# Sum of absolute differences: absolute sums moved to ScalarE, the last row cut into column pieces, six buffers

## The chip, the cores and the metric

The kernel runs on one core of one Trainium2 chip. The metric is the device time of one execution in microseconds (us). TensorE does no work in this kernel; what matters are the transfers from HBM (the chip's main memory) into SBUF (the core's working memory of 128 partitions), VectorE (DVE in the rows), ScalarE (ACT) and SyncE (SP). DMAs can be issued from SP and from ACT; each has a queue of its own, SPq and ACTq in the rows, and the packets of both run on the core's 16 DMA engines.

## The reference

Two float32 arrays of 1024 x 4096 are subtracted, and the absolute differences are summed along each row. The result is one float32 for each of the 1024 rows.

```python
batch, dim = 1024, 4096          # x, y: float32, axis = -1
return np.sum(np.abs(x - y), axis=axis).astype(np.float32)
```

The inputs are 2 x 16.78 MB, the output 4 KB.

## The kernel before

The 1024 rows are laid over the 128 partitions, eight to each partition. The loop (line 29) runs over these eight slots. The text calls a slot a "row": row 0 to row 7, each a tile of 128 x 4096 of x and one of y, 2 MB apiece.

For each row, SP issues the transfer of the x tile (line 33) and ACT that of the y tile (line 34). VectorE subtracts in place, tx = tx - ty (line 35), and then sums the absolute values of tx along the free dimension into one column of `ro` (line 36). After the loop SP writes `ro` out (line 38). ScalarE computes nothing; only its queue is used.

The pools for x and y have four buffers each (lines 23 and 24), so the first four rows are issued at once and the transfer of row 4 has to wait until row 0 has been used: its y transfer until the subtraction has read ty, its x transfer until the absolute sum has read tx. The order on VectorE is made by a scheduler that does not keep the order of the loop: it puts two subtractions and then two sums, as the rows of VectorE's order further down show.

Of the kernel before, what the change touches and what calls it, by code (L numbers as in the profile page):

```python
# [5 lines left out]

KCS = [1]*8

@with_exitstack
def kernel(ctx, tc, x, y, axis, out):  # L10
    nc = tc.nc
    P = nc.NUM_PARTITIONS
    R, C = x.shape
    K = R // P
    xr = x.rearrange("(p k) c -> p k c", p=P, k=K)
    yr = y.rearrange("(p k) c -> p k c", p=P, k=K)
    orr = out.rearrange("(p k) -> p k", p=P, k=K)
    kcs = KCS
    assert sum(kcs) == K
    pools = {}  # L20
    for kc in set(kcs):
        pools[kc] = (
            ctx.enter_context(tc.tile_pool(name=f"px{kc}", bufs=4)),
            ctx.enter_context(tc.tile_pool(name=f"py{kc}", bufs=4)),
        )
    with tc.tile_pool(name="pr", bufs=1) as poolr:
        ro = poolr.tile([P, K], mybir.dt.float32)
        o = 0
        for kc in kcs:
            poolx, pooly = pools[kc]  # L30
            tx = poolx.tile([P, kc, C], x.dtype)
            ty = pooly.tile([P, kc, C], y.dtype)
            nc.sync.dma_start(out=tx, in_=xr[:, o:o+kc, :])
            nc.scalar.dma_start(out=ty, in_=yr[:, o:o+kc, :])  # L34
            nc.vector.tensor_sub(out=tx, in0=tx, in1=ty)  # L35
            nc.vector.reduce_sum(out=ro[:, o:o+kc], in_=tx, axis=mybir.AxisListType.X, apply_absolute_value=True)  # L36
            o += kc
        nc.sync.dma_start(out=orr, in_=ro)


# [1 line left out]
_INS = ['x', 'y', 'axis']  # L42
_OUTS = [((1024,), 'float32')]
#: Inputs that are plain numbers.
_NUMBERS = {'axis': -1}


def kernel(**inputs):
    import numpy as _np
    import concourse.bacc as _bacc  # L50
    import concourse.tile as _tile
    from concourse import mybir as _mybir
    from concourse.bass_utils import run_bass_kernel_spmd as _run

    nc = _bacc.Bacc("TRN2", target_bir_lowering=False, num_devices=1)  # L55
    arrays, args = {}, []
    for name in _INS:
        if name in _NUMBERS:
            args.append(_NUMBERS[name])
            continue  # L60
        a = _np.ascontiguousarray(inputs[name])
        if a.dtype.kind in "iu":
            a = a.astype(_np.int64)
        arrays[f"in_{name}_dram"] = a
        args.append(nc.dram_tensor(f"in_{name}_dram", a.shape, _mybir.dt.from_np(a.dtype), kind="ExternalInput").ap())
    for i, (shape, dtype) in enumerate(_OUTS):
        dt = _mybir.dt.from_np(_np.dtype(dtype))
        args.append(nc.dram_tensor(f"out_{i}_dram", shape, dt, kind="ExternalOutput").ap())
    with _tile.TileContext(nc) as tc:
        kernel(tc, *args)  # L70
    r = _run(nc, [arrays], core_ids=[0])
    got = tuple(r.results[0][f"out_{i}_dram"] for i in range(len(_OUTS)))
    return got[0]
```

## Time and profile before

| | |
|---|---|
| median of 3 runs | 97.60 us (97.56 to 97.62) |
| span of the profiled execution, first to last instruction | 95.8 us |
| VectorE busy | 69.9 us, 73% of the span, 16 instructions |
| one subtraction / one absolute sum of 128 x 4096 | 4.42 us / 4.41 us |
| bytes read from HBM | 33.55 MB |
| rate of the transfers while they run | 424 to 433 GB/s |

The whole time of the profiled execution is not listed apart from the three runs, which lie within 0.06 us. It is taken as their median: 97.6 us, of which the span is 95.8 us, and the other 1.8 us lie around the span.

A row of the profile names the line, the engine, the operation and its tiles. Idle time of an engine is put down to what ended it. The time of a DMA "to landing" runs from its issue to the moment at which its semaphore says that all of it is there.

### The profile page before, as it was taken

What the parts mean: (1) busy time and instruction counts of PE and PEld (TensorE: products, weight loads), DVE (VectorE), ACT (ScalarE), POOL (GpSimd) and SP (SyncE); (2) the same over time, 40 slices, a digit from 0 to 9 for tenths busy, and PEclk for the clock granted to TensorE, in tenths of its full rate; (3) what the DMA queues carried; (4) which work ended last, traced back from release to release, by engine and by line L of the source; (5) the groups of instructions that cost most, each with busy time, mean ns of one, the idle gap of its engine ahead of it and who ended that gap; (6) DMA issues with size and microseconds to landing.
All of it is one profiled execution on the core that took longest, in us unless ns stands there. A gap on an engine that the chain in (4) does not pass through costs nothing.

```text
span 95.8 us, 95 instructions
## 1 busy us (share of the span) xinstructions
DVE 69.9 (73%) x16; POOL 0.2 (0%) x4
## 2 busy tenths in 40 slices
DVE  0000069996930499999982999999909999999990
POOL 0000000000000000000000000000000000000000
DMA  4899999999999999999999999999999995000000
GB/s 109 369 431 424 424 438 438 438 431 438 431 424 438 424 417 431 431 411 431 438 438 424 431 431 431 424 424 424 431 411 438 438 438 212 0 0 0 0 0 2
DMA packets 2448, 33.56 MB, mean 350 GB/s; under 512 B 400, under 2 KB 400, under 8 KB 400
## 3 DMA queue, kind: packets, MB, share of 16 engines
q1 hardware_dynamic: 1296, 16.78, 41.7%
q10 hardware_dynamic: 1152, 16.78, 41.1%
HBM read 33.55 MB, written 0.00 MB: 350 GB/s over the span
## 4 chain that ended last, share of the span: by engine, by line
DMA 68%; DVE 24%; issue 4%; ACTq 1%
DMA ty<-in_y_dram 68%; DVE tx L35 14%; DVE ro L36 10%; ACTq L34 1%
## 5 line engine op out<-in xcount | busy, mean ns | idle before, releaser
L35 DVE TENSOR_TENSOR tx<-tx,ty 128x4096 f32<-128x4096 f32 x8 | 35.4, 4422 | 23.6 <-DMA ty<-in_y_dram 23.6
L36 DVE TENSOR_REDUCE ro<-tx 128x1 f32<-128x4096 f32 x8 | 35.1, 4413 | 0.1
L55 POOL MEMSET const-bfloat16-1.0<- 128x1 bf16 x1 | 0.1, 103 | 0.0
L55 POOL MEMSET const-uint8-127<- 128x1 uint8 x1 | 0.1, 103 | 0.0
L55 POOL MEMSET const-float32-1.0<- 128x1 f32 x1 | 0.1, 100 | 0.0
L55 POOL MEMSET const-float32-0.0<- 128x1 f32 x1 | 0.1, 99 | 0.2 <-issue 0.2
## 6 DMA issues: line engine op xcount, KB each, us to landing
ty<-in_y_dram ACTq DMA_DIRECT2D x8, 2048.0 KB, 33.1
tx<-in_x_dram SPq DMA_DIRECT2D x8, 2048.0 KB, 23.6
out_dram<-ro SPq DMA_DIRECT2D x1, 4.0 KB, 1.4
```

The costliest lines, as they stand in the source:

```text
L34: nc.scalar.dma_start(out=ty, in_=yr[:, o:o+kc, :])
L35: nc.vector.tensor_sub(out=tx, in0=tx, in1=ty)
L36: nc.vector.reduce_sum(out=ro[:, o:o+kc], in_=tx, axis=mybir.AxisListType.X, apply_absolute_value=True)
L55: nc = _bacc.Bacc("TRN2", target_bir_lowering=False, num_devices=1)
```

## The change

VectorE now only subtracts. The absolute sums of whole rows are ScalarE activations with the function Abs, which also accumulate along the free dimension into a column of `ro`. The pools have six buffers. The order is the order of the code (`manual_schedule`): loads of rows 0 to 3, then for each row the load of the row four ahead, the subtraction and the absolute sum.

Row 7 is cut into column pieces of 2304, 1152, 512 and 128. All eight of its transfers (x and y of each piece) are issued on SP's queue. Each of the first three pieces is subtracted on VectorE and summed on ScalarE into one of three columns of a small tile `last`. The fourth piece, 128 columns, is subtracted into the same tile beside these three columns, and one VectorE reduction over the 131 columns of `last` gives the sum of row 7.

```diff
-KCS = [1]*8
+PIECES = [2304, 1152, 512, 128]
...
-            ctx.enter_context(tc.tile_pool(name=f"px{kc}", bufs=4)),
-            ctx.enter_context(tc.tile_pool(name=f"py{kc}", bufs=4)),
...
+    px = ctx.enter_context(tc.tile_pool(name="px", bufs=6))
+    py = ctx.enter_context(tc.tile_pool(name="py", bufs=6))
+    ps = ctx.enter_context(tc.tile_pool(name="ps", bufs=1))
+    with tc.manual_schedule():
+        ro = ps.tile([P, K], F32, tag="ro")
+        last = ps.tile([P, n_part + PIECES[-1]], F32, tag="last")
...
+            if k < K - 1:
+                nc.sync.dma_start(out=tx, in_=xr[:, k, :])
+                nc.scalar.dma_start(out=ty, in_=yr[:, k, :])
+                return
+            o = 0
+            for w in PIECES:
+                nc.sync.dma_start(out=tx[:, o:o + w], in_=xr[:, k, o:o + w])
+                nc.sync.dma_start(out=ty[:, o:o + w], in_=yr[:, k, o:o + w])
+                o += w
...
+            nc.vector.tensor_sub(out=tx, in0=tx, in1=ty)
+            nc.scalar.activation(tx, tx, ABS, accum_out=ro[:, k:k + 1])
...
+        for k in range(4):
+            load(k)
+        for k in range(K - 1):
+            if k + 4 < K:
+                load(k + 4)
+            whole(k)
...
-            nc.vector.tensor_sub(out=tx, in0=tx, in1=ty)
-            nc.vector.reduce_sum(out=ro[:, o:o+kc], in_=tx, axis=mybir.AxisListType.X, apply_absolute_value=True)
...
+        for i, w in enumerate(PIECES):
+            s = slice(o, o + w)
+            if i < n_part:
+                nc.vector.tensor_sub(out=tx[:, s], in0=tx[:, s], in1=ty[:, s])
+                nc.scalar.activation(tx[:, s], tx[:, s], ABS, accum_out=last[:, i:i + 1])
+            else:
+                nc.vector.tensor_sub(out=last[:, n_part:n_part + w], in0=tx[:, s], in1=ty[:, s])
+                nc.vector.reduce_sum(out=ro[:, K - 1:K], in_=last, axis=AX, apply_absolute_value=True)
```

VectorE's order before, from row 0 to the end. A name with DMAHW in the brackets is a semaphore that counts landed DMAs; DVE and Activation are the semaphores of VectorE and ScalarE.

```order
L35 TENSOR_TENSOR tx<-tx,ty 128x4096
L36 TENSOR_REDUCE ro<-tx 128x1
L35 TENSOR_TENSOR tx<-tx,ty 128x4096 x2
L36 TENSOR_REDUCE ro<-tx 128x1 x2
L35 TENSOR_TENSOR tx<-tx,ty 128x4096 x2
L36 TENSOR_REDUCE ro<-tx 128x1 x2
L35 TENSOR_TENSOR tx<-tx,ty 128x4096 x2
L36 TENSOR_REDUCE ro<-tx 128x1 x2
L35 TENSOR_TENSOR tx<-tx,ty 128x4096
L36 TENSOR_REDUCE ro<-tx 128x1
```

Behind the last subtraction but one stand two sums, and only then the subtraction and the sum of row 7. VectorE's order in the change, from the subtraction of row 6 to the end:

```order
L50 TENSOR_TENSOR tx<-tx,ty 128x4096 [waits DMAHW5_49,DMAHW4_49,Activation_49]
L64 TENSOR_TENSOR tx<-tx,ty 128x2304 [waits DMAHW7_49,DMAHW6_49,Activation_49]
L64 TENSOR_TENSOR tx<-tx,ty 128x1152 [waits DMAHW1_49,DMAHW0_49]
L64 TENSOR_TENSOR tx<-tx,ty 128x512 [waits DMAHW3_49,DMAHW2_49]
L67 TENSOR_TENSOR last<-tx,ty 128x128 [waits DMAHW5_49,DMAHW4_49]
L68 TENSOR_REDUCE ro<-last 128x1 [waits DVE_49,Activation_49]
```

The sums are gone from VectorE up to the last reduction, which now waits for ScalarE. ScalarE's order in the change, behind the first four issues of y transfers (before, it had eight issues of y transfers and nothing else):

```order
L40 DMA ty_85<-in_y_dram 128x4096 [waits DMAHW0_49]
L51 ACT_TABLE_LOAD
L51 ACTIVATE tx_68,ro_66<-tx_68 128x4096 [waits DVE_49]
L40 DMA ty_91<-in_y_dram 128x4096 [waits DMAHW3_49]
L51 ACTIVATE tx_72,ro_66<-tx_72 128x4096 [waits DVE_49]
L40 DMA ty_97<-in_y_dram 128x4096 [waits DMAHW5_49]
...
L51 ACTIVATE tx_96,ro_66<-tx_96 128x4096 [waits DVE_49]
L65 ACTIVATE tx_102,last_67<-tx_102 128x2304 [waits DVE_49]
L65 ACTIVATE tx_102,last_67<-tx_102 128x1152 [waits DVE_49]
L65 ACTIVATE tx_102,last_67<-tx_102 128x512 [waits DVE_49]
```

tx_68 is row 0, tx_72 row 1, tx_96 row 6 and tx_102 row 7; the y transfers shown are those of rows 4, 5 and 6. The issues of rows 5 and 6 now stand behind an activation. SP's order in the change, behind the x transfers of rows 0 to 5 (before, it had eight transfers of 128 x 4096 and the output):

```order
L39 DMA tx<-in_x_dram 128x4096 [waits DMAHW4_49,Activation_49]
L44 DMA tx<-in_x_dram 128x2304 [waits DMAHW6_49,Activation_49]
L45 DMA ty<-in_y_dram 128x2304 [waits DMAHW7_49,DVE_49]
L44 DMA tx<-in_x_dram 128x1152 [waits DMAHW0_49]
L45 DMA ty<-in_y_dram 128x1152 [waits DMAHW1_49]
L44 DMA tx<-in_x_dram 128x512 [waits DMAHW2_49]
L45 DMA ty<-in_y_dram 128x512 [waits DMAHW3_49]
L44 DMA tx<-in_x_dram 128x128 [waits DMAHW4_49]
L45 DMA ty<-in_y_dram 128x128 [waits DMAHW5_49]
L70 DMA out_dram<-ro 128x8 [waits DMAHW6_49,DVE_49]
```

The eight DMA semaphores are used in turn, so a transfer also waits for the one that used its semaphore eight transfers earlier: the pieces of 1152 columns for row 4, those of 512 for row 5, those of 128 for row 6.

## Rows read from the trace of the kernel before

**Rows 1.** The page's busy times, then the chain that ended last, by engine.
```profile
DVE 69.9 (73%) x16; POOL 0.2 (0%) x4
...
DMA 68%; DVE 24%; issue 4%; ACTq 1%
```

**Rows 2.** Stretches: from:to and length, VectorE and GpSimd busy, TensorE clock, DMA share, GB/s.
```profile
12.92:22.72 9.80, 8.85 (x2) 0.00 (x0) 1.00 1.01 433
61.90:71.70 9.80, 7.61 (x2) 0.00 (x0) 1.00 1.01 430
71.70:80.30 8.60, 8.60 (x2) 0.00 (x0) 1.00 1.00 425
80.30:81.46 1.16, 1.16 (x2) 0.00 (x0) 1.00 0.01 0
81.46:93.60 12.14, 12.07 (x3) 0.00 (x0) 1.00 0.00 0
```

**Rows 3.** Timeline, start to row 2: start, length, engine, line, operation, idle before.
```profile
0.72 0.39 ACTq L34 DMA_DIRECT2D ty<-in_y_dram  x1
...
12.92 4.43 DVE L35 TENSOR_TENSOR tx<-tx,ty 128x4096 f32<-128x4096 f32 x1 [12.92 <-DMA ty<-in_y_dram]
17.38 0.34 ACTq L34 DMA_DIRECT2D ty<-in_y_dram  x1
...
21.83 0.33 SPq L33 DMA_DIRECT2D tx<-in_x_dram  x1
...
32.51 4.43 DVE L35 TENSOR_TENSOR tx<-tx,ty 128x4096 f32<-128x4096 f32 x1 [5.37 <-DMA ty<-in_y_dram]
```

**Rows 4.** Timeline from the issue of row 7's transfers to the end.
```profile
49.96 0.33 ACTq L34 DMA_DIRECT2D ty<-in_y_dram  x1
...
52.10 4.42 DVE L35 TENSOR_TENSOR tx<-tx,ty 128x4096 f32<-128x4096 f32 x1 [2.17 <-DMA ty<-in_y_dram]
...
60.88 0.33 SPq L33 DMA_DIRECT2D tx<-in_x_dram  x1
...
71.70 4.43 DVE L35 TENSOR_TENSOR tx<-tx,ty 128x4096 f32<-128x4096 f32 x1 [2.19 <-DMA ty<-in_y_dram]
76.04 8.74 DVE L36 TENSOR_REDUCE ro<-tx 128x1 f32<-128x4096 f32 x2
84.70 4.42 DVE L35 TENSOR_TENSOR tx<-tx,ty 128x4096 f32<-128x4096 f32 x1
89.15 4.42 DVE L36 TENSOR_REDUCE ro<-tx 128x1 f32<-128x4096 f32 x1
93.60 0.35 SPq L38 DMA_DIRECT2D out_dram<-ro  x1
```

**Rows 5.** Issue to landing (the last column, us): row 0's y, row 7's, the output.
```profile
ty<-in_y_dram ACTq DMA_DIRECT2D x1, 2048.0 KB, 12.2
...
ty<-in_y_dram ACTq DMA_DIRECT2D x1, 2048.0 KB, 31.5
...
tx<-in_x_dram SPq DMA_DIRECT2D x1, 2048.0 KB, 20.4
...
out_dram<-ro SPq DMA_DIRECT2D x1, 4.0 KB, 1.4
```

**Rows 6.** Groups: form and count | busy us, mean ns | idle before and releaser.
```profile
L35 DVE TENSOR_TENSOR tx<-tx,ty 128x4096 f32<-128x4096 f32 x8 | 35.4, 4422 | 23.6 <-DMA ty<-in_y_dram 23.6
L36 DVE TENSOR_REDUCE ro<-tx 128x1 f32<-128x4096 f32 x8 | 35.1, 4413 | 0.1
L55 POOL MEMSET const-float32-0.0<- 128x1 f32 x1 | 0.1, 99 | 0.2 <-issue 0.2
```

29 lines of the change are left out of this document (14 added, 15 removed).

## The prediction

> **What bounds the kernel now.** I read the busy times and the chain of waits first. VectorE is busy for 69.9 of 95.8 us, and the chain is 68% DMA and 24% VectorE [rows 1]. So there are two limits, one after the other, and the stretches tell where they change. From 3 us on the 16 DMA engines are full: a row of x and y takes 9.80 us at 430 to 433 GB/s, DMA share 1.01 [rows 2]. VectorE needs 4.42 + 4.41 = 8.83 us for a row [rows 6], less than 9.80, so up to row 6 it waits for data: 2.19 us just before the subtraction at 71.70 [rows 4]. Bytes stop at 80.30 [rows 2]. The last transfers land at 49.96 + 31.5 = 81.46 (y) and 60.88 + 20.4 = 81.28 (x) [rows 4, 5].
>
> What is left then is a backlog. At 71.70 VectorE still owes the sum of row 5, because its order puts two sums behind the subtraction of row 6. So 4.43 us of subtraction, 8.74 us of two sums, 4.42 and 4.42 us for row 7 run without a gap to 93.57 [rows 4], 12.1 us after all data is there. The output is issued at 93.60, and the span ends 2.20 us later. The median of the runs is 97.6, so 1.8 us lie around the span.
>
> **The change part by part.** *Transfers up to row 6.* Same bytes, same two queues. Six buffers and earlier issues can bring nothing here, as the DMA share is 1.00 to 1.01 from 12.92 to 80.30 [rows 2]. They may cost something if a queue runs dry. SP's x of row 5 now waits for a landing of row 1 (about 22.7, one row after 12.92), its x of row 6 for row 2 (32.51, [rows 3]) and for the first activation. On ACT, the y transfer of row 5 stands behind the table load and the activation of row 0, that of row 6 behind the activation of row 1. At sum price (4.41 us, below) row 0's activation ends at 12.92 + 4.43 + 4.41 = 21.8, row 1's at 31.6. The queue ahead of row 5's y holds row 4's y, which lands at 52.10 [rows 4]: about 30 us of cover. I cost all of this at 0. For the table load no row has a price; it has the 4.43 us of the first subtraction to hide in, and behind that 5.4 us in every row (9.80 - 4.41), so that tens of us would not reach row 6. Row 6 lands at 71.70 as before.
>
> *Row 7's transfers.* They follow row 6 on SP's queue alone. Four pieces of x and y, of 56.25%, 28.1%, 12.5% and 3.1% of the row. The row takes 71.70 to 81.46 = 9.76 us, so at the old rate the pieces land at 77.19, 79.94, 81.16 and 81.46. Their issues don't hold them up: the smallest pieces wait for row 6's landing at 71.70, when 84% of the row (the first two pieces, 8.2 us of transfer) is already queued, and eight issues of 0.33 us [rows 4] are 2.6 us. Smaller packets and a single queue have no row; from below 0 (the packets already fill the engines), from above the half-rate rival below.
>
> *VectorE.* The 8 sums of 4.41 us leave it. Subtractions at 4422 ns per 4096 columns: row 6 from 71.70 to 76.13, the pieces 2.49, 1.24, 0.55 and 0.14 us. They end at 77.19 + 2.49 = 79.68, 79.94 + 1.24 = 81.18, 81.73 and 81.87. VectorE is not the limit.
>
> *ScalarE.* Its price for an absolute sum is in no row. The nearest is VectorE's sum of the same elements, 4.413 us for 4096 columns, and I take that: 4.41 us for row 6, 2.48, 1.24 and 0.55 us for the three pieces. Row 6 starts at 76.15 and ends at 80.56, so piece 1 (ready at 79.68) waits 0.9 us for it. Then they run in a line: 83.04, 84.28, 84.83. That is where the time ends: ScalarE is 3 us behind the data. The last reduction of 131 columns, 4413 x 131 / 4096 = 0.14 us, ends at 84.97; five handovers at the 0.02 to 0.03 us seen between 93.57 and 93.60 make it 85.05. The output tail of 2.23 us (93.57 to 95.80) gives a span of 87.3, and 1.8 around it 89.1 us.
>
> Bounds of that price. If ScalarE cost nothing, the last piece decides: 81.87 + 0.14 + 2.23 + 1.8 = 86.05. At twice the price row 6 would end at 84.97, the pieces at 93.5, and the time would be 93.5 + 0.14 + 0.1 + 2.23 + 1.8 = 97.8, the time before. A fixed cost per instruction that my price per column leaves out: the shortest row of any engine is 0.099 us, a one-element fill on GpSimd [rows 6]; four instructions on the path after row 6 make +0.4 us. As much in the other direction is a tenth less for each column (0.97 instead of 1.08 ns, over 4096 + 3968 columns 0.9 us). Nothing favours either side, so I take the sum with no correction, rounded down to 89.0.
>
> The Trainium skill has a price: ScalarE: Activation LUTs, section What ACT_TABLE_LOAD costs, gives about 280 ns plus 0.833 ns per column for an ACTIVATE, says nothing of what accumulating adds, and puts a switch of tables at 2.66 us. By it row 6 would cost 3.69 us and the pieces 2.20, 1.24 and 0.71, ending the time at an estimated 88.2 instead of 89.1. No row here shows an activation.
>
> **The rivals.** *The last landing decides.* If ScalarE takes at most half of VectorE's price, its line ends with the last subtraction, near 81.9, and the time is 86.1. For it: nothing in the rows prices ScalarE. Against it: both VectorE operations cost 1.08 ns per column, and this would be 0.54. Values between half and full price lie between 86.1 and 89.1.
>
> *A single queue is slower.* Before, both queues always had work; no row has one alone. If SP's queue alone got half of the rate, row 7 would take 19.5 us and land at 91.2. The last subtraction, the third activation (piece 3 lands at 90.6, 0.55 subtract, 0.55 sum, 91.7) and the reduction end at 91.85, the time is 95.9. Against it: the share of the 16 engines is 1.01 with two queues, so packets follow each other without overlapping, and one queue should fill the same places. A tenth less rate lands the row 1.0 us later, but only 0.1 us of it reaches ScalarE, since piece 1 (0.6 us later) is ready 0.9 us before ScalarE is.
>
> *The small transfers pay one after another.* This one ends on the slower side. Row 0's y took 12.2 us from issue to landing, of which the bytes of row 0 are 9.80: 2.4 us of fixed delay [rows 3, 5]. If the eight transfers of row 7 don't overlap in it, seven times 2.4 = 16.8 us are added, the last lands at 98.3, ScalarE is long done, and the time is 98.3 + 0.14 + 0.14 + 2.23 + 1.8 = 102.6. It decides from 1.6 us for each transfer: (97.6 - 1.8 - 2.23 - 0.28 - 81.46) / 7. Against it: on each queue of the kernel before, one transfer follows the other with no gap at the row's end (9.80 us for every row, 1.01 share), so the delay overlaps when transfers are queued ahead, as these are.
>
> The rule behind it is in the Trainium skill, DMA: Bandwidth & Descriptors, Rules for kernel authors: for the full rate at least 1 MiB in a DMA, and under 64 KB mostly overhead. Of the eight transfers two have more than 1 MiB; those of 512 columns have 256 KiB, those of 128 exactly 64 KiB. No run here shows such a size.
>
> *ScalarE is over twice as dear.* Then the new tail is longer than the old one: over 97.8, and from 2.2 times on (9.80 / 4.41) it falls behind in every row. It ends slower too. For it: an in-place write of the whole row besides the sum, and a line of four activations at the end. Against it: VectorE's subtraction writes the whole row as well and costs the same as the sum that writes one column (4422 and 4413 ns, [rows 6]).
>
> *The change doesn't do what it says.* The deeper buffers may move no transfer, as the semaphores used in turn hold the fifth row until the first has landed. That costs nothing: the engines are full either way, and the time is that of the forecast.
>
> **How the numbers follow.** Forecast (ScalarE's line ends last, at 0.8 to 1.2 of VectorE's price): 0.78, time 89.0. The last landing decides: 0.10, 86.1 to 87.0. Single queue much slower: 0.05, up to 95.9. Small transfers in turn: 0.03, slower. ScalarE over twice: 0.03, slower; around exactly twice it would be the same time, 0.01. Within the forecast, 0.8 of the price (3.53 for row 6, so that piece 1 starts at 79.70, and 3.42 for the pieces) ends the line at 83.12 and the time at 87.4; 1.1 of it ends at 81.00 + 4.70 = 85.70 and 90.0, and the fixed costs add up to 0.4. The range is 87.0 to 90.6. A measurement of this kernel can tell 0.2%, 0.2 us, from no change. Faster 0.93, same 0.01, slower 0.06.
>
> **What would show it right or wrong.** Right: the subtraction of row 6 starts at 71.7 after a wait for a DMA; the first piece's subtraction waits for its DMA and starts near 77.2; the activations of row 6 and of the three pieces stand without gaps; the last reduction waits for ScalarE, not for a DMA, for about 3 us; the output is issued near 85.1. Wrong: the last reduction follows its subtraction at once (ScalarE cheap, or the landing late); DMA share under 0.9 between 72 and 80 (single queue, small packets); activations longer than 5 us; the subtraction of any row up to 6 later than before (a queue ran dry behind an activation).

## The result and the profile after

The changed kernel takes 88.28 us (median of 4 runs, 88.26 to 88.32); the kernel before 97.61 us (97.56 to 97.62). The ratio is 0.9045, with a 95% interval of 0.9032 to 0.9058: 9.3 us are gone. The forecast was 89.0 us.

The page of the changed kernel, its busy times and the chain by engine, against [rows 1]:

```profile
DVE 36.1 (42%) x12; ACT 31.1 (36%) x21; POOL 0.2 (0%) x4
...
DMA 81%; ACT 9%; DVE 5%; SPq 1%; issue 0%; ACTq 0%; DVEq 0%
```

VectorE's 24% of the chain are now 5%, ScalarE has 9%, the transfers 81%. VectorE's work is halved, but that is not the gain by itself, as the experiments show.

The stretches of the changed kernel (from:to and length, busy VectorE, ScalarE and GpSimd, TensorE clock, DMA share, GB/s), which answer to [rows 2]:

```profile
12.92:71.70 58.78, 26.55 (x6) 23.54 (x13) 0.00 (x0) 1.00 1.00 427
71.70:77.00 5.30, 4.42 (x1) 0.72 (x1) 0.00 (x0) 1.00 1.00 419
77.00:80.30 3.30, 2.83 (x2) 3.30 (x3) 0.00 (x0) 1.00 1.01 399
80.30:81.50 1.20, 1.17 (x2) 1.20 (x1) 0.00 (x0) 1.00 0.59 186
```

The transfers are as they were up to 71.70, and the DMA share is 1.00 or 1.01 up to 80.30. In the last row, on one queue and in smaller packets (the page counts 3312 packets where it counted 2448 before, for the same 33.56 MB), the rate falls a little, from 427 to 419 and 399 GB/s. Some bytes still move behind 80.30, where before none did [rows 2].

What a sum costs on ScalarE, which no row of before could show (form and count | busy us, mean ns | idle before and releaser; against the 4413 ns of [rows 6]):

```profile
L51 ACT ACTIVATE tx<-tx 128x4096 f32<-128x4096 f32 x7 | 25.3, 3616 | 39.5 <-DVE tx L50 39.5
L64 DVE TENSOR_TENSOR tx<-tx,ty 128x2304 f32<-128x2304 f32 x1 | 2.6, 2557 | 1.0 <-DMA ty<-in_y_dram 1.0
L65 ACT ACTIVATE tx<-tx 128x2304 f32<-128x2304 f32 x1 | 2.1, 2107 | 0.0
L64 DVE TENSOR_TENSOR tx<-tx,ty 128x1152 f32<-128x1152 f32 x1 | 1.4, 1358 | 0.3 <-DMA ty<-in_y_dram 0.3
L51 ACT ACTIVATION_READ_ACCUMULATOR tx<-tx 128x1 f32 x7 | 1.3, 187 | 0.0
L51 ACT ACT_TABLE_LOAD x1 | 1.3, 1283 | 13.3 <-DMA ty<-in_y_dram 13.3
L65 ACT ACTIVATE tx<-tx 128x1152 f32<-128x1152 f32 x1 | 1.1, 1147 | 0.0
L64 DVE TENSOR_TENSOR tx<-tx,ty 128x512 f32<-128x512 f32 x1 | 0.7, 691 | 0.0
L65 ACT ACTIVATE tx<-tx 128x512 f32<-128x512 f32 x1 | 0.6, 613 | 0.0
```

The code has one activation where the chip runs two instructions: the activation, and a read of the accumulator of 187 ns. The two overlap, so that together they take 3.71 us for 4096 columns.

The timeline of the end, against [rows 4]:

```profile
71.82 4.42 DVE L50 TENSOR_TENSOR tx<-tx,ty 128x4096 f32<-128x4096 f32 x1 [5.44 <-DMA ty<-in_y_dram]
...
76.28 3.62 ACT L51 ACTIVATE tx<-tx 128x4096 f32<-128x4096 f32 x1 [6.15 <-DVE tx L50]
77.20 2.56 DVE L64 TENSOR_TENSOR tx<-tx,ty 128x2304 f32<-128x2304 f32 x1 [0.96 <-DMA ty<-in_y_dram]
79.80 0.19 ACT L51 ACTIVATION_READ_ACCUMULATOR tx<-tx 128x1 f32 x1
79.89 2.11 ACT L65 ACTIVATE tx<-tx 128x2304 f32<-128x2304 f32 x1
80.02 2.08 DVE L64 TENSOR_TENSOR tx<-tx,ty 128x1152 f32<-128x1152 f32 x2 [0.27 <-DMA ty<-in_y_dram]
81.90 0.19 ACT L65 ACTIVATION_READ_ACCUMULATOR tx<-tx 128x1 f32 x1
82.00 1.15 ACT L65 ACTIVATE tx<-tx 128x1152 f32<-128x1152 f32 x1
82.02 0.28 DVE L67 TENSOR_TENSOR last<-tx,ty 128x128 f32<-128x128 f32 x1
...
83.14 0.61 ACT L65 ACTIVATE tx<-tx 128x512 f32<-128x512 f32 x1
83.66 0.19 ACT L65 ACTIVATION_READ_ACCUMULATOR tx<-tx 128x1 f32 x1
83.88 0.29 DVE L68 TENSOR_REDUCE ro<-last 128x1 f32<-128x131 f32 x1 [1.58 <-ACT tx L65]
84.20 0.35 SPq L70 DMA_DIRECT2D out_dram<-ro  x1
```

From 76.28 to 83.85 ScalarE works without a gap, and VectorE's last reduction, whose own subtraction ended at 82.30, waits 1.58 us for it. But VectorE's subtraction of the first piece ends at 79.76 (77.20 + 2.56), only 0.13 us before ScalarE starts to sum that piece. Two chains arrive there almost together, and a chain of waits can show only one.

Where the last row landed. First the issues of its four y transfers, in the timeline, then their time to landing in us (the last column), against [rows 4, 5]:

```profile
42.77 0.39 SPq L45 DMA_DIRECT2D ty<-in_y_dram  x1
...
52.47 0.42 SPq L45 DMA_DIRECT2D ty<-in_y_dram  x1
...
62.07 0.43 SPq L45 DMA_DIRECT2D ty<-in_y_dram  x1
...
71.88 0.43 SPq L45 DMA_DIRECT2D ty<-in_y_dram  x1
```

```profile
ty<-in_y_dram SPq DMA_DIRECT2D x1, 1152.0 KB, 34.3
...
ty<-in_y_dram SPq DMA_DIRECT2D x1, 576.0 KB, 27.5
...
ty<-in_y_dram SPq DMA_DIRECT2D x1, 256.0 KB, 19.2
...
ty<-in_y_dram SPq DMA_DIRECT2D x1, 64.0 KB, 9.8
```

The pieces land at 77.1, 80.0, 81.3 and 81.7, the sums of the two. Before, row 7 was complete at 81.46. So the smaller transfers and the single queue cost at most 0.2 us; row 6's subtraction too starts 0.1 us later than before (71.82 against 71.70).

### The profile page after: what moved, and what is told of

Its sections match the earlier page's. It is cut to its first block, busy times and chain, and to the rows that moved or that the text cites. A ratio compares the mean times of both kernels' runs of the same rounds, so it can differ in the third digit from the quotient of the medians.

```text
span 86.5 us, 117 instructions
## 1 busy us (share of the span) xinstructions
DVE 36.1 (42%) x12; ACT 31.1 (36%) x21; POOL 0.2 (0%) x4
## 2 busy tenths in 40 slices
DMA packets 3312, 33.56 MB, mean 388 GB/s; under 512 B 496, under 2 KB 752, under 8 KB 1264
## 3 DMA queue, kind: packets, MB, share of 16 engines
q1 hardware_dynamic: 2304, 18.88, 52.6%
## 4 chain that ended last, share of the span: by engine, by line
DMA 81%; ACT 9%; DVE 5%; SPq 1%; issue 0%; ACTq 0%; DVEq 0%
DMA ty<-in_y_dram 45%; DMA tx<-in_x_dram 36%; DVE tx L50 5%; ACT tx L65 4%; ACT tx L51 4%; SPq L39 1%; DVE ro L68 0%; ACTq L101 0%; DVEq L50 0%
## 5 line engine op out<-in xcount | busy, mean ns | idle before, releaser
L50 DVE TENSOR_TENSOR tx<-tx,ty 128x4096 f32<-128x4096 f32 x7 | 31.0, 4425 | 45.3 <-DMA ty<-in_y_dram 45.3
L51 ACT ACTIVATE tx<-tx 128x4096 f32<-128x4096 f32 x7 | 25.3, 3616 | 39.5 <-DVE tx L50 39.5
L51 ACT ACT_TABLE_LOAD x1 | 1.3, 1283 | 13.3 <-DMA ty<-in_y_dram 13.3
L64 DVE TENSOR_TENSOR tx<-tx,ty 128x2304 f32<-128x2304 f32 (+2 forms) x3 | 4.6, 1535 | 1.3 <-DMA ty<-in_y_dram 1.2
L65 ACT ACTIVATE tx<-tx 128x2304 f32<-128x2304 f32 (+2 forms) x3 | 3.9, 1289 | 0.0
L51 ACT ACTIVATION_READ_ACCUMULATOR tx<-tx 128x1 f32 x7 | 1.3, 187 | 0.0
L65 ACT ACTIVATION_READ_ACCUMULATOR tx<-tx 128x1 f32 x3 | 0.6, 187 | 0.0
```

What stands on the lines that cost most here:

```text
L51: nc.scalar.activation(tx, tx, ABS, accum_out=ro[:, k:k + 1])
L64: nc.vector.tensor_sub(out=tx[:, s], in0=tx[:, s], in1=ty[:, s])
L65: nc.scalar.activation(tx[:, s], tx[:, s], ABS, accum_out=last[:, i:i + 1])
```

## The experiments

The theory: the time is set by what stands behind the last data on the engine that ends last, and in the changed kernel that is ScalarE's line. The main rival: the last landing. All ratios are to the kernel before, on the same chip, with their 95% intervals. By these intervals, 0.13 us either way, two versions less than 0.2 us apart can't be told from each other.

**The order alone.**

```diff
-        for kc in kcs:
...
+    with tc.manual_schedule():
...
+        for k in range(4):
+            load(k)
+        for k in range(K):
+            tx, ty = tiles[k]
             nc.vector.tensor_sub(out=tx, in0=tx, in1=ty)
-            nc.vector.reduce_sum(out=ro[:, o:o+kc], in_=tx, axis=mybir.AxisListType.X, apply_absolute_value=True)
-            o += kc
+            nc.vector.reduce_sum(out=ro[:, k:k+1], in_=tx, axis=mybir.AxisListType.X, apply_absolute_value=True)
+            if k + 4 < K:
+                load(k + 4)
```

> The kernel before with its four buffers and its VectorE sums, but in the order of the code: subtract, sum, subtract, sum. Theory (what counts is the work that stands behind the last data): row 6 is subtracted 71.70 to 76.13 and summed to 80.55, so VectorE is free when row 7 lands at 81.46; 4.42 + 4.41 us more end at 90.3, and with 2.23 us of output and 1.8 us around the span the time is 94.3 us. Rival (VectorE has the same 16 operations, so their order moves nothing): 97.6 us.

94.40 us, ratio 0.9671 (0.9658 to 0.9685). Its timeline at the end:

```profile
76.28 4.42 DVE L42 TENSOR_REDUCE ro<-tx 128x1 f32<-128x4096 f32 x1
81.59 4.42 DVE L41 TENSOR_TENSOR tx<-tx,ty 128x4096 f32<-128x4096 f32 x1 [0.90 <-DMA ty<-in_y_dram]
86.05 4.42 DVE L42 TENSOR_REDUCE ro<-tx 128x1 f32<-128x4096 f32 x1
```

VectorE now waits 0.90 us for row 7, where before it came to it 3.2 us late (84.70 against 81.46, [rows 4, 5]). The same 16 operations in another order give 3.2 of the 9.3 us.

**Pieces without ScalarE.**

```diff
-            nc.scalar.activation(tx, tx, ABS, accum_out=ro[:, k:k + 1])
+            nc.vector.reduce_sum(out=ro[:, k:k + 1], in_=tx, axis=AX, apply_absolute_value=True)
...
-                nc.scalar.activation(tx[:, s], tx[:, s], ABS, accum_out=last[:, i:i + 1])
+                nc.vector.reduce_sum(out=last[:, i:i + 1], in_=tx[:, s], axis=AX, apply_absolute_value=True)
```

> The changed kernel with all absolute sums back on VectorE; pieces, order and six buffers stay. Theory (one engine for both operations cannot use the early landing of the pieces): row 6's sum ends at 80.7, then piece 1 costs 2.56 + 2.56 us, piece 2 2.7, piece 3 1.4, piece 4 0.6: last reduction ends at 90.5, time 94.5 us, as with whole rows in this order. Rival (the pieces alone bring the gain): about 88 us.

94.28 us, 0.9662 (0.9649 to 0.9675): within 0.2 us of the order alone. VectorE is still summing row 6 when the first piece lands near 77.2, and from then on it has no gap:

```profile
76.32 4.42 DVE L51 TENSOR_REDUCE ro<-tx 128x1 f32<-128x4096 f32 x1
80.65 2.55 DVE L64 TENSOR_TENSOR tx<-tx,ty 128x2304 f32<-128x2304 f32 x1
...
89.99 0.29 DVE L68 TENSOR_REDUCE ro<-last 128x1 f32<-128x131 f32 x1
```

**ScalarE without pieces.**

```diff
-            if k < K - 1:
+            if k < K:
                 nc.sync.dma_start(out=tx, in_=xr[:, k, :])
                 nc.scalar.dma_start(out=ty, in_=yr[:, k, :])
...
-        for k in range(K - 1):
+        for k in range(K):
...
-        for i, w in enumerate(PIECES):
...
```

Row 7 goes whole, x on SP's queue and y on ACT's, and the code for the pieces is left out.

> The changed kernel without pieces: row 7 is loaded, subtracted and summed whole, sums on ScalarE. Theory: row 7 lands at 81.5 to 81.7, subtraction to 86.0, activation 3.62 and its read 0.19 us to 89.8, time 93.8 us. Rival (taking the sums off VectorE brings the gain): about 88 us.

93.79 us, 0.9610 (0.9597 to 0.9623). VectorE waits 5.33 us for row 7, and then its subtraction and ScalarE's sum stand one behind the other:

```profile
81.59 4.42 DVE L49 TENSOR_TENSOR tx<-tx,ty 128x4096 f32<-128x4096 f32 x1 [5.33 <-DMA ty<-in_y_dram]
86.05 3.62 ACT L50 ACTIVATE tx<-tx 128x4096 f32<-128x4096 f32 x1 [6.05 <-DVE tx L49]
```

So, on top of the order, ScalarE alone is worth 0.6 us and the pieces alone 0.1, too little to be told from nothing, but both together 6.1 us (94.40 to 88.28). These runs also have six buffers where the order run has four, which the next run shows to make no difference in the changed kernel. Each takes away what makes the other useless: the busy engine when the piece arrives, and the wait for the whole row.

**Four buffers.**

```diff
-    px = ctx.enter_context(tc.tile_pool(name="px", bufs=6))
-    py = ctx.enter_context(tc.tile_pool(name="py", bufs=6))
+    px = ctx.enter_context(tc.tile_pool(name="px", bufs=4))
+    py = ctx.enter_context(tc.tile_pool(name="py", bufs=4))
```

> The changed kernel with four buffers instead of six. Theory (the DMA engines are full with four): 88.3 us, no change. Rival (the deeper buffers keep the queues filled while issues stand behind activations on ScalarE's queue): slower by 1 us or more, with a DMA share under 0.95 somewhere between 13 and 72 us.

88.23 us, 0.9047 (0.9034 to 0.9059), the changed kernel's time. The y transfer of row 5 is issued later (27.21 instead of 22.52), and the stretch before row 6 is as full as with six:

```profile
12.92:71.70 58.78, 26.55 (x6) 23.53 (x13) 0.00 (x0) 1.00 1.00 427
```

**Two sums of the last row left out.** ScalarE doesn't sum the pieces of 1152 and 512 columns; their two columns of `last` are set to zero at the start.

```diff
+        nc.vector.memset(last[:, 1:n_part], 0.0)
...
-                nc.scalar.activation(tx[:, s], tx[:, s], ABS, accum_out=last[:, i:i + 1])
+                if i == 0:
+                    nc.scalar.activation(tx[:, s], tx[:, s], ABS, accum_out=last[:, i:i + 1])
```

> The changed kernel without ScalarE's sums of the pieces of 1152 and 512 columns (their two columns of the small tile are set to zero at the start; the sums of row 7 lack them). Theory (ScalarE's line ends last): the last reduction then waits for the sum of the first piece, which ends near 82.1, and for VectorE's own subtraction of the last piece, which ends at 82.30; it runs to 82.6 instead of 84.17, time 86.7 us. Rival (the last landing decides): 88.3 us, no change.

86.84 us, 0.8895 (0.8882 to 0.8907). The last transfer lands where it did (81.72 against 81.68) and the time falls by 1.44 us, close to the 1.58 us that the reduction had waited. In the changed kernel it is ScalarE's line, not the landing, that ends last. Here ScalarE is done at 82.11, and the reduction follows VectorE's own last subtraction:

```profile
82.07 0.28 DVE L69 TENSOR_TENSOR last<-tx,ty 128x128 f32<-128x128 f32 x1
82.46 0.29 DVE L70 TENSOR_REDUCE ro<-last 128x1 f32<-128x131 f32 x1
```

So with these four pieces the landing and VectorE would allow 86.84 us.

**Row 6's sum left out.** Its column of `ro` is set to zero at the start.

```diff
+        nc.vector.memset(ro[:, K - 2:K - 1], 0.0)
...
-            nc.scalar.activation(tx, tx, ABS, accum_out=ro[:, k:k + 1])
+            if k < K - 2:
+                nc.scalar.activation(tx, tx, ABS, accum_out=ro[:, k:k + 1])
```

> The changed kernel without ScalarE's sum of row 6 (its output column is set to zero). The chain of waits of the changed kernel runs through this activation (3.71 us). Theory after the profile (it ties with the subtraction of the first piece, which ends at 79.76 and lets its activation start 0.1 us later at the earliest): only about 0.1 us, time 88.2 us. Rival (the prediction's step: row 6's sum holds the first piece by 0.9 us): 87.4 us. Naive reading of the chain: 3.7 us less, 84.6 us.

88.15 us, 0.9034 (0.9022 to 0.9046). A sum of 3.71 us that stands in the chain of waits gives back 0.13 us when it goes, which is too little to be told from nothing. Close behind it stood the subtraction of the first piece:

```profile
77.14 2.56 DVE L66 TENSOR_TENSOR tx<-tx,ty 128x2304 f32<-128x2304 f32 x1 [0.97 <-DMA ty<-in_y_dram]
79.73 2.12 ACT L67 ACTIVATE tx<-tx 128x2304 f32<-128x2304 f32 x1 [9.66 <-DVE tx L66]
```

ScalarE had been idle for 9.66 us and still could not start before 79.73, against 79.89 in the changed kernel. Of these 0.16 us, 0.06 are an earlier start of the subtraction (77.14 against 77.20).

**One queue for everything.**

```diff
-                nc.scalar.dma_start(out=ty, in_=yr[:, k, :])
+                nc.sync.dma_start(out=ty, in_=yr[:, k, :])
```

> The changed kernel with all transfers, the y rows too, on SP's queue. Theory (the 16 engines are full with one queue as with two; the changed kernel's row 7 moved at 419 GB/s on SP's queue alone, 425 before): 88.3 to 88.7 us. Rival (a single queue is slower): 2 to 5% of 78 us of transfers, 90 us or more.

88.26 us, 0.9050 (0.9035 to 0.9065), no change. One queue moves 427 GB/s up to row 6, as two do:

```profile
12.92:71.70 58.78, 26.55 (x6) 22.26 (x12) 0.00 (x0) 1.00 1.00 427
```

**A version from the theory.** Row 6 goes in two halves, so that ScalarE starts earlier; row 7 in smaller first pieces; and VectorE sums the last two pieces together with the four partial sums. The tile `six` holds the two sums of row 6's halves, which VectorE adds.

```diff
-PIECES = [2304, 1152, 512, 128]
+PIECES = [1024, 1024, 1024, 512, 384, 128]
+ON_ACT = 4
+HALF = 2048
...
+            if k == K - 2:
+                for h in range(2):
+                    s = slice(h * HALF, (h + 1) * HALF)
+                    nc.vector.tensor_sub(out=tx[:, s], in0=tx[:, s], in1=ty[:, s])
+                    nc.scalar.activation(tx[:, s], tx[:, s], ABS, accum_out=six[:, h:h + 1])
+                return
...
```

> A version to beat both, from the theory: row 6 subtracted and summed in two halves, so that ScalarE starts 2.2 us earlier; row 7 in pieces of 1024, 1024, 1024, 512, 384 and 128 columns, the last two summed by VectorE with the four partial sums. Theory (ScalarE's line decides): ScalarE ends row 6 near 78.2, then the four pieces at 79.3, 80.4, 81.5 and 82.2; the last two pieces are subtracted by 82.1 and the reduction of 516 columns takes 0.69 us: ends at 82.9 instead of 84.17, time 87.0 us. Rival (small transfers pay): 12 transfers instead of 8 in the last row land it later, 88.3 us or more.

87.38 us, 0.8953 (0.8941 to 0.8965): faster than both kernels, though 0.4 us short of what was expected. The two halves and pieces bring ScalarE's end down to 82.23 (82.04 + 0.19); now VectorE ends last. It has to wait for the landing once more, at 81.66, and the reduction is longer:

```profile
81.66 0.76 DVE L80 TENSOR_TENSOR last<-tx,ty 128x384 f32<-128x384 f32 x2 [0.38 <-DMA ty<-in_y_dram]
82.04 0.19 ACT L75 ACTIVATION_READ_ACCUMULATOR tx<-tx 128x1 f32 x1
82.52 0.69 DVE L82 TENSOR_REDUCE ro<-last 128x1 f32<-128x516 f32 x1
```

**Each half of that version by itself**, first the halves of row 6 with the four old pieces:

> The changed kernel with its four pieces, and only row 6 subtracted and summed in two halves. Theory (the first piece's subtraction ends at 79.76 at the earliest and then holds ScalarE, whatever row 6 does): 88.2 to 88.3 us. Rival (row 6's activation alone holds ScalarE's line): ScalarE is free at 78.3 instead of 80.0, time 86.6 us.

88.24 us, 0.9039 (0.9027 to 0.9052): no change. ScalarE is done with row 6 at 78.34 and then idles 1.45 us until the subtraction of the large first piece is over:

```profile
78.15 0.19 ACT L56 ACTIVATION_READ_ACCUMULATOR tx<-tx 128x1 f32 x1
79.79 2.12 ACT L73 ACTIVATE tx<-tx 128x2304 f32<-128x2304 f32 x1 [1.45 <-DVE tx L72]
```

Then the six pieces with row 6 whole:

> The changed kernel with only the six pieces of the balanced version; row 6 whole. Theory: ScalarE is free at 80.0 and then sums 1024, 1024, 1024 and 512 columns one after the other, 81.1, 82.1, 83.1 and 83.8; the reduction of 516 columns (0.69 us) ends at 84.6 instead of 84.17, time 88.7 us: slower than the four pieces. Rival (finer pieces help by themselves, as the data is used earlier): 87.4 us as in the balanced version.

88.61 us, 0.9077 (0.9065 to 0.9090): 0.3 us slower than the change. The first pieces wait for ScalarE, which is busy with row 6 until 80.0; the reduction waits 1.27 us for it and is longer by 0.4 us than the one of 131 columns:

```profile
83.76 0.69 DVE L73 TENSOR_REDUCE ro<-last 128x1 f32<-128x516 f32 x1 [1.27 <-ACT tx L68]
```

Singly the two parts bring 0.0 and -0.3 us (the longer reduction is 0.4 of it), together 0.9 us: where two chains nearly tie, shortening one gives nothing until the other is shortened too.

**A shorter end.** In the balanced version:

```diff
-PIECES = [1024, 1024, 1024, 512, 384, 128]
+PIECES = [1280, 1024, 896, 512, 256, 128]
```

> The balanced version with pieces of 1280, 1024, 896, 512, 256 and 128 columns. In the balanced version VectorE ends last: it subtracts 384 and 128 columns once they have landed (81.66 to 82.42) and reduces 516 columns in 0.69 us. Theory: 256 columns less 128 to subtract after the landing and a reduction of 388 columns (0.56 us) end 0.25 us earlier, time 87.1 us. Rival (ScalarE's line of four pieces ends last here, as the bytes moved to it cost as much): 87.4 us, no change.

87.18 us, 0.8933 (0.8921 to 0.8945): the fastest of all, though the 0.2 us below the version that it was made from are at the limit of what can be told (runs of 87.16 to 87.30 against 87.34 to 87.44, and the two intervals overlap by 0.0004). The two engines now end together, VectorE's subtractions at 82.50 and ScalarE's read at 82.54:

```profile
81.85 0.65 DVE L80 TENSOR_TENSOR last<-tx,ty 128x256 f32<-128x256 f32 x2
82.35 0.19 ACT L75 ACTIVATION_READ_ACCUMULATOR tx<-tx 128x1 f32 x1
82.60 0.56 DVE L82 TENSOR_REDUCE ro<-last 128x1 f32<-128x388 f32 x1
```

## Why the prediction was right, and where its size was off

**What bounded the kernel before** was read rightly: full transfers up to 80.30, a last landing at 81.46, and a backlog on VectorE. The prediction named the scheduler's order as the reason for the backlog, but gave it no price of its own; it is 3.2 us of it.

**The transfers up to row 6**: costed at 0. Row 6's subtraction starts at 71.82, before at 71.70, and neither four buffers nor one queue move the time. That the issues of two y transfers stand behind activations cost nothing, as the 30 us of cover said. The table load, 1283 ns, ran while ScalarE waited for the first subtraction.

**Row 7's landings**: forecast 77.19, 79.94, 81.16 and 81.46; by the issues and times above 77.1, 80.0, 81.3 and 81.7. The fixed delay of the small transfers overlaps, as argued.

**VectorE**: the first piece's subtraction was to end at 79.68 and ended at 79.76. The price per column left out a fixed part: 2557, 691 and 284 ns for 2304, 512 and 128 columns, where it gave 2487, 553 and 138. Nothing waited for most of it. The last reduction, 0.29 us where it gave 0.14, does stand at the end of the path.

**ScalarE's line** was the right place, and its price was the term of the sum that was mis-sized. VectorE's 4.41 us for a row stood in for 3.71 us. The whole line, row 6 and three pieces, was forecast from 76.15 to 84.83, 8.68 us, and ran from 76.28 to 83.85, 7.57 us. From that follow the other misses: the first piece was to wait 0.9 us for ScalarE and waited 0.13, so that the line was no longer one chain but two in a near tie, and VectorE's reduction waited 1.58 us instead of 3 (0.4 of the difference is its own subtraction, which ended at 82.30 instead of 81.87). The last reduction ended at 84.17 instead of 85.05; with 2.3 us to the end of the span and 1.8 around it, as before, that is 88.3 instead of 89.1.

That the miss is no larger owes something to luck. The prediction weighed two corrections, +0.4 us for a fixed part of four instructions and -0.9 us for a tenth less per column, and took neither, though by its own numbers they don't balance. Both turned out about twice as large. Between 512 and 2304 columns an activation grows by 0.83 ns per column (613 to 2107 ns) where VectorE's sum takes 1.08, which is some 2.0 us less over the 8064 columns of the line. What is left is some 0.2 us for each of the four sums, 0.8 us more. The 1.1 us by which the line was too long are the difference.

The estimate from the Trainium skill (ScalarE: Activation LUTs, What ACT_TABLE_LOAD costs) came to 88.2 and was closer, in part by luck. The Trainium skill gives the 280 ns there, to which 0.833 ns per column are added, for an activation whose bias is a pointer operand, and 186 ns for one with immediate scale and bias. The trace agrees with the second: by it 4096, 2304, 1152 and 512 columns take 3598, 2105, 1146 and 612 ns, and the rows have 3616, 2107, 1147 and 613. The read of the accumulator, which the estimate did not have, ends 0.09 us behind each activation, and that is about what the first price has too much. The Trainium skill's 1283 ns for the load of a table is the trace's number; the rest of its 2.66 us for a switch no run here shows.

**The rivals.** The last landing: refuted by leaving out two sums, which moved the end by 1.44 us under the same transfers. It sets the floor, though. The prediction put that floor at 86.05; the run without the two sums puts it at 86.84 for the four pieces, since the last landing is 0.2 us later and each subtraction and the reduction have a fixed part. The fastest version is 0.3 us above. The single queue: full, and the same time with all transfers on it. Small transfers one after another: they landed 0.2 us later, not 16.8. The 1.6 us for each transfer from which the prediction let this rival decide is where the time would be that of before again; by its own sum the landing would end last from some 0.5 us on. Likewise, of a tenth less rate it let 0.1 us reach ScalarE, where its own numbers leave none (piece 1 would be 0.6 us later, with 0.9 us of room). ScalarE over twice as dear: 0.84 of VectorE. The deeper buffers: no effect, as said.

What the prediction did not see is how little each part does alone. It reckoned the whole change in one sum, and that was enough for the time, but a reader could take from it that moving the sums to ScalarE was the gain. By itself that is worth 0.6 us after the order is fixed.

## What to carry to other kernels

When a kernel is full of transfers up to its last byte, as this one is, the work behind that byte is what can still be shortened: order the engines so that nothing older is pending then, cut the last tile so that its work starts before it has all landed, and give its steps to engines that can run beside each other. Such parts do not add up, so one that gives nothing alone is not thereby useless, and what stands in the chain of waits gives back only as much as the next chain leaves. For an operation that no row shows, the nearest row of another engine was 19% too high here (4.41 us for 3.71); the time came within 1% because only 8.7 of 89 us hung on that price. Half and twice the price told beforehand which way the place of the wait could tip.

## What the runs showed that was not expected

- ScalarE's sum with an accumulator is two instructions, 3616 and 187 ns for 4096 columns, overlapping by some 0.09 us; together they are 16% shorter than VectorE's 4413 ns.
- One queue fills the 16 engines: 427 GB/s on SP's queue alone from 12.92 to 71.70, the same as on two.
- The last bytes and the last landing did not move together. Before, bytes stop at 80.3 us and the landing comes at 81.46; in the changed kernel, with small transfers at the end, bytes stop near 81.1 and the landing comes at 81.68, so 0.8 us more of transfer cost 0.2 us. Why the landing follows sooner no run shows.
- A profile shows one run, and it need not be the median one: with everything on one queue the profiled run took 88.58 us and the other three 88.23 to 88.27. So the output's issue at 84.50 there, 0.3 us later than in the changed kernel (84.20), says nothing against the equal medians (88.26 and 88.28).
